# The gating branch's v projection as seven block products, with block sums of its weights made by accumulating transfers

## The chip, the core and the metric

The kernel runs on one core of a Trainium2 chip. The core's engines work side by side and meet through semaphores: TensorE (PE) does the matmuls and transposes, ScalarE (ACT) and VectorE (DVE) work on tiles in SBUF and PSUM, GpSimd (POOL) builds masks and issues accumulating transfers, and SyncE (SP) issues loads. The metric is the device time of one execution in microseconds (us); lower is better. All inputs and outputs are float32.

## The reference, cut to what matters

One decoder layer for 512 tokens of width 1024: one input projection of x feeds a gated branch (gMLP) and a sparse attention of three branches, both are projected and merged, and a channel mixer with two layer norms follows. What the change touches is the gated branch's v:

```
z = x @ w_in                        # columns 0:1024 are u, 1024:2048 are v
u, v = split(gelu(z[:, :2048]), 2)
v = layer_norm(v, gm_ln_g, gm_ln_b) # then a causal 128 x 128 mix over positions, per group
y_gm = u * (W_s v + b)
...
k_cmp, v_cmp = compress(z_kc), compress(z_vc)    # the stage that follows v
f = square(relu(h @ w_ff1)) @ w_ff2              # made with seven products for 3 of 4 quarters
```

## The kernel before

**Precision.** Each float32 matmul is three matmuls on split operands. `split` (L142) makes a hi part of a weight tile on ACT (L150) and the remainder lo on DVE (L151); `xh` and `xl` are the same split of x^T, made out of PSUM after PE's transposes (L339 to L344). A product is hi x hi, hi x lo and lo x hi.

**The weight stream.** `Stream` (L40 to L98) holds two lists: chunks, which are loads into a ring of buffers (L80, issued by SP), and items, which are splits of a chunk or of a part of it. A chunk's load can be issued once the last item of the chunk that held its buffer has been split. The ring `raw` has two buffers; the hi and lo tiles have three each. `ws.get` hands out the next item and prepares two more ahead. Rings `V` and `S`, in a pool that opens only for the channel mixer, serve FF2.

**The order of the work.** The program is written in the order of the stages; around v that is: x transposed and u's first six columns (L347 to L366, order written out by hand), u's last two columns (L372 to L378), v (L403 to L418), small transposes of constants (L432 to L441), the projections kc and vc (L442 to L451), the compression (L454 to L460). Outside the parts under `manual_schedule` a scheduler places the instructions of each engine in an order of its own, fixed when the kernel is built; on the chip each engine then runs its list strictly in order and waits where an operand or a buffer is late.

**v.** Two column halves of 512. For each, eight contraction blocks k times four token tiles t, with x^T's 128 x 128 blocks stationary and 512 weight columns moving, three matmuls each: 2 x 8 x 4 x 3 = 192 matmuls into four PSUM banks. ACT evicts with gelu into `v`, DVE collects `bn_stats`. The weights come as eight chunks of 512 KB, each split in one go. After v, ACT issues the loads of the compression's weights, `cw1_0` and `cw1_1`, 2 MB each (L420 to L423); constants for the gated branch (`gmc`, three rows spread over all partitions, and `misc`) are loaded from ACT's queue while u ends (L385 to L398).

**FF2.** For three of the four quarters of w_ff2, `du_chunks`, `du_item` and `s13` (L211 to L248) make seven products out of blocks. The weight is cut into blocks W(k, c), contraction half k and column half c, each further into two parts h. Chunk U holds W11 and W22, V holds W21, S holds W12 twice. `s13` adds U to both copies of S; later S is added to U and U to V. Each addition is a transfer of 512 KB from SBUF to SBUF that POOL issues with `accum_op=add` (L207). `ff2_product` (L854) multiplies in the order 1, 2, 6, 5, 7, 3, 4 and adds each product's bank into `hn`.

**Masks.** The attention pool `apool` opens at the start; POOL makes the distance masks `Bm` and `Dc` in it, and ACT scales `Bm`'s four slices during u (L365).

Of the kernel before, what the change touches and what calls it, by code (L numbers as in the profile page):

```python
# [16 lines left out]
P = 128  # L17
# [83 lines left out]
def layer_kernel(ctx: ExitStack, tc: tile.TileContext, x, w_in, gm_ln_g, gm_ln_b, gm_w_s, gm_b_s,  # L101
# [66 lines left out]
    def rows_b(src, ks, c0, ncol, per_piece=1, dst=None):  # L168
        for k in ks[::2]:
# [5 lines left out]
    add(**dict(shape=[1, 768], dmas=[(lambda t: t, wv[:, 0:1, 0:768])],  # L175
                       pieces=[((lambda t, j=j: t[:, 0, 384 * j:384 * j + 384]), None) for j in range(2)]))
    add(**dict(shape=[1, 768], dmas=[(lambda t: t, wv[:, 1:2, 0:768])],
                       pieces=[((lambda t: t[:, 0]), None)]))
    rows_b(wv, list(range(2, 8)), 0, 768)
    cols_a(w_in, 768, 256)  # L180
    for h in range(2):
        rows_b(wv, list(range(8)), C_V + 512 * h, 512, per_piece=2)
    cols_a(w_in, C_KC, 512)
    cols_a(w_in, C_KS, 256)
    cols_a(w_in, C_KW, 256)
    for k in range(0, 8, 2):
        add(**dict(
            shape=[2, 536],
            dmas=[(lambda t: t[:, :, 0:256], wv[:, k:k + 2, C_VS:C_VS + 256]),
                  (lambda t: t[:, :, 256:536], wv[:, k:k + 2, C_VW:C_VW + 280])],  # L190
            pieces=[((lambda t, j=j: t[:, j]), None) for j in range(2)]))
    cols_a(w_pg, 0, 1024)
    cols_a(w_in, C_Q, 1024)
    cols_a(w_in, C_ZM, 2048)
    cols_a(w_pn, 0, 1024)
    res = {}
    w_ov = w_o.rearrange("(k p) c -> p k c", p=P)
    rows_b(w_ov, [0, 1], 0, 1024)
    rows_b(w_ov, [2, 3, 4, 5], 0, 1024, dst=lambda k: (res["oh"][:, k - 2], res["ol"][:, k - 2]))
    rows_b(w_ov, [6, 7], 0, 1024)  # L200
    w2v = w2.rearrange("(k p) c -> p k c", p=P)
    w1v = w1.rearrange("(k p) c -> p k c", p=P)
    for name in "VS":
        ws.ring(name, 2, lambda shape, n, tag=name: res["lpool"].tile([P] + shape, F32, tag=tag, bufs=2, name=n),
                ready=lambda: "rings" in res)
# [5 lines left out]
    def du_chunks(shape, blk):  # L211


        one, two = (lambda t: t[:, 0]), (lambda t: t[:, 1])
        return dict(U=ws.chunk("raw", [2] + shape, [(two, blk(0, 0)), (one, blk(1, 1))]),
                    V=ws.chunk("V", shape, [((lambda t: t), blk(0, 1))]),
                    S=ws.chunk("S", [2] + shape, [(one, blk(1, 0)), (two, blk(1, 0))]))

    def ff2_blocks(q, h):
        def blk(half, k):  # L220
            k0 = 8 * q + 4 * k + 2 * h
            return w2v[:, k0:k0 + 2, 512 * half:512 * half + 512]
        return du_chunks([2, 512], blk)
# [25 lines left out]
    FF2 = (1, 2, 6, 5, 7, 3, 4)  # L249
# [11 lines left out]
    for q in range(4):  # L261
        for i, c in enumerate((0, 512, 256, 768)):
            cols_a(w1, 1024 * q + c, 256, ring="S" if q and i < 2 else "raw",
                   dsts=((early, early if i == 0 else None) if q == 0 and i < 2 else (None, None)))
        if q < 3:
            dus = [ff2_blocks(q, h) for h in range(2)]
            for p in FF2:
                for h in range(2):
                    du_item(dus[h], p, s13(dus[h]) if p == 1 else None)
# [15 lines left out]
    for c, (c0, c1) in enumerate(((0, 128), (128, 256), (256, 512), (512, 768), (768, 1024))):  # L285
# [3 lines left out]
    att = ctx.enter_context(ExitStack())  # L289
    apool = att.enter_context(tc.tile_pool(name="apool", bufs=1))  # L290
    Kh = apool.tile([P, 2, 1056], F32R, name="Kh")
    Kl = apool.tile([P, 2, 1056], F32R, name="Kl")
    Vch = apool.tile([32, 2, HD], F32R, name="Vch")
    Vcl = apool.tile([32, 2, HD], F32R, name="Vcl")
    Bm = apool.tile([P, 4, 512], F32, name="Bm")
    Dm = Bm[:, 0]
    nc.gpsimd.iota(Dm, pattern=[[-1, 512]], base=384, channel_multiplier=1,
                   allow_small_or_imprecise_dtypes=True)
    nc.gpsimd.affine_select(Dm, Dm, pattern=[[-1, 512]], compare_op=ALU.is_ge, fill=BIG,
                            base=384, channel_multiplier=1)  # L300
    Dc = apool.tile([P, 4, 32], F32, name="Dc")
    nc.gpsimd.iota(Dc, pattern=[[128, 4], [-16, 32]], base=-15, channel_multiplier=1,
                   allow_small_or_imprecise_dtypes=True)
    nc.vector.tensor_scalar(Dc, Dc, -0.5, None, op0=ALU.add)
    nc.gpsimd.affine_select(Dc, Dc, pattern=[[128, 4], [-16, 32]], compare_op=ALU.is_ge, fill=BIG,
                            base=-31, channel_multiplier=1)
# [30 lines left out]
    uT = slab("uT", [P, 8, S])  # L337

    def x_transpose(k):  # L339
        pt = bank("d")  # L340
        for t in range(4):
            nc.tensor.transpose(pt[:, t * P:(t + 1) * P], xn[:, t, k * P:(k + 1) * P], ident)
        nc.scalar.activation(xh[:, k], pt, AF.Copy)
        nc.vector.tensor_sub(xl[:, k], pt, xh[:, k].bitcast(F32))  # L344

    ub = [bank(t) for t in BANKS[:6]]
    with tc.manual_schedule():  # L347
        ws.prep(0)
        x_transpose(0)
        for k in range(8):  # L350
            if k == 0:
# [12 lines left out]
            if k in (3, 4, 5, 6):  # L364
                nc.scalar.activation(Bm[:, 6 - k], Dm, AF.Copy, scale=2.0 ** (k - 7))  # L365
    for c in range(6):  # L366
        nc.scalar.activation(uT[:, c], ub[c], AF.Gelu_apprx_tanh)

# [5 lines left out]
    for c in range(6, 8):  # L374
        pc = ws.get()
        ps = bank("d")
        dense_a(ps, pc, xh, xl)
        nc.scalar.activation(uT[:, c], ps, AF.Gelu_apprx_tanh)  # L378

# [24 lines left out]
    for h in range(2):  # L404
        vb = [bank(t) for t in (BANKS[:4] if h == 0 else BANKS[4:])]
        for kk in range(4):
            hi, lo = ws.get()
            for j in range(2):
                k = 2 * kk + j
                for t in range(4):  # L410
                    ts_ = slice(t * P, (t + 1) * P)
                    nc.tensor.matmul(vb[t], xh[:, k, ts_], hi[:, j], start=k == 0, stop=False)  # L412
                    nc.tensor.matmul(vb[t], xl[:, k, ts_], hi[:, j], start=False, stop=False)  # L413
                    nc.tensor.matmul(vb[t], xh[:, k, ts_], lo[:, j], start=False, stop=k == 7)  # L414
        for t in range(4):
            vs_ = v[:, t, h * 512:(h + 1) * 512]
            nc.scalar.activation(vs_, vb[t], AF.Gelu_apprx_tanh)
            nc.vector.bn_stats(st6[:, t, h], vs_)  # L418
    cw1 = []
    for i, w in enumerate((cmp_w1_k, cmp_w1_v)):  # L420
        t = slab(f"cw1_{i}", [P, 32, HD])
        nc.scalar.dma_start(t, w[0].rearrange("(l d) e -> d l e", d=HD))
        cw1.append(t)  # L423

# [379 lines left out]
    def block(t, i):  # L804
        return t[:, i].rearrange("p (k t) -> p k t", k=4)

# [47 lines left out]
    def ff2_product(q, p):  # L854

        where = {1: "A", 2: "B", 5: "C", 6: "A", 3: "C", 7: "A", 4: "A"}[p]
        opens = p in (1, 2, 5)
        if opens:
            g2[where] = [bank(t) for t in {"A": "dd", "B": "aa", "C": "ac"}[where]]
        for h in range(2):  # L860
            hi, lo = ws.get()
            for j in range(2):
                js = slice(j * P, (j + 1) * P)
                ps = g2[where][j]
                for kk in range(2):
                    yh, yl = (y[:, 2 * h + kk, js] for y in Y[p])
                    nc.tensor.matmul(ps, yh, hi[:, kk], start=opens and h == 0 and kk == 0, stop=False,  # L867
                                     skip_group_check=True)
                    nc.tensor.matmul(ps, yl, hi[:, kk], start=False, stop=False, skip_group_check=True)  # L869
                    nc.tensor.matmul(ps, yh, lo[:, kk], start=False, stop=h == 1 and kk == 1,  # L870
                                     skip_group_check=True)
        half, e, sign, first = {1: (0, 0, 1, 1), 2: (0, 0, 1, 0), 6: (1, 0, 1, 1), 5: (1, 1, -1, 1),
                                7: (1, 1, -1, 0), 3: (1, 0, 1, 0), 4: (0, 1, -1, 1)}[p]
        for j in range(2):
            v = hn[:, 2 * half + j, e * 512:(e + 1) * 512]
            nc.vector.scalar_tensor_tensor(v, v, ALPHA if q == 0 and first else 1.0, g2[where][j],
# [7 lines left out]
    for q in range(4):  # L884
# [17 lines left out]
        if q < 3:  # L902
            for p in FF2:
                ff2_product(q, p)
# [44 lines left out]
```

## Time and profile before

| what | us |
|---|---|
| median of 3 runs | 893.12 |
| lowest, highest run | 891.62, 894.25 |
| the profiled execution, its own time | 893.99 |
| its span in the trace | 892.3 |
| u, its first and last matmul's start | 7.45, 55.35 |
| v, its first and last matmul's start | 55.58, 98.87 |
| small transposes, the first one's start | 99.19 |
| kc, its first matmul's start | 100.27 |

The span runs from the first to the last recorded instruction; the time of the execution is a little longer. A matmul's recorded duration (0.39 us) is longer than its distance to the next one, because matmuls overlap in the array: rates are read from the starts.

### The profile page before, as it was taken

To read this page: it belongs to the slowest core of one execution; us is meant where nothing else is said; L and a number is where in the kernel's file an instruction comes from. 1 tells how busy PE (TensorE), PEld (TensorE's weight loads), DVE (VectorE), ACT (ScalarE), POOL (GpSimd) and SP (SyncE) were. 2 spreads that over 40 slices of the span, in tenths; PEclk is the share of its full clock that TensorE was granted. 3 is DMA by queue.
4 is the path that set the end of the run, shared out by engine and by line. 5 is a ranking of instruction groups with operands and counts; after the bars stand their busy time and mean duration, and the time that the engine had idled before them with its cause. 6 is when DMAs were issued, how large, how long until landed. Compare 5 with 4: busy or idle time off the path is not lost.

```text
span 892.3 us, 10986 instructions
## 1 busy us (share of the span) xinstructions
PE 878.0 (98%) x4288; PEld 734.0 (82%) x4288; DVE 500.4 (56%) x977; ACT 367.8 (41%) x644; POOL 24.3 (3%) x36
## 2 busy tenths in 40 slices
PE   8999999999999999999999999999999999999995
PEld 6888898998888788888878888888888888888884
DVE  3423654542236866766745688457457635853457
ACT  3522322342234655656633412554355345535500
POOL 1000000000000000000000000010011001100000
PEclk9999999999999999999999999999999999999998
DMA  6467520143331111121135441666557738541401
GB/s 203 127 196 204 175 72 25 51 157 100 106 100 57 48 48 48 48 94 49 41 118 195 165 142 42 194 147 183 188 148 136 235 125 183 114 146 48 142 24 71
DMA packets 70772, 104.78 MB, mean 117 GB/s; under 512 B 2432, under 2 KB 50368, under 8 KB 70720
## 3 DMA queue, kind: packets, MB, share of 16 engines
q1 hardware_dynamic: 62752, 83.99, 29.1%
q0 software_dynamic: 3456, 12.58, 7.5%
q10 hardware_dynamic: 4512, 7.50, 2.7%
q8 instruction: 33, 0.54, 0.3%
q14 instruction: 19, 0.16, 0.0%
HBM read 89.39 MB, written 2.10 MB: 103 GB/s over the span
## 4 chain that ended last, share of the span: by engine, by line
PE 97%; DVE 1%; DMA 1%; ACT 0%; issue 0%; SPq 0%; DVEq 0%; ACTq 0%
PE ps L133 19%; PE ps L135 19%; PE ps L134 19%; PE ps L867 4%; PE ps L870 4%; PE ps L869 4%; PE ps L737 3%; PE ps L735 3%; PE ps L736 3%; PE ps L662 2%; PE ps L414 2%; PE ps L412 2%; PE ps L457 2%; PE ps L413 2%; PE ps L677 1%; PE ps L679 1%
## 5 line engine op out<-in xcount | busy, mean ns | idle before, releaser
L151 DVE TENSOR_TENSOR wlo<-raw,whi 128x1024 fp32r<-128x1024 f32 (+3 forms) x118 | 136.6, 1162 | 196.2 <-ACT whi L150 192.7
L150 ACT ACTIVATE whi<-raw 128x1024 fp32r<-128x1024 f32 (+3 forms) x118 | 118.9, 1011 | 234.2 <-PE ps L134 154.1
L133 PE MATMUL ps<-xh,whi 128*128 128x512 f32 x320 | 129.4, 404 | 0.0
L135 PE MATMUL ps<-xh,wlo 128*128 128x512 f32 x320 | 125.8, 393 | 0.0
L134 PE MATMUL ps<-xl,whi 128*128 128x512 f32 x320 | 125.8, 393 | 0.0
L133 PE MATMUL ps<-hTh,whi 128*128 128x512 f32 x232 | 90.3, 389 | 0.0
L134 PE MATMUL ps<-hTl,whi 128*128 128x512 f32 x232 | 90.3, 389 | 0.0
L135 PE MATMUL ps<-hTh,wlo 128*128 128x512 f32 x232 | 90.3, 389 | 0.0
L135 PEld LDWEIGHTS ps<-xh,wlo 128*128 128x128 f32 x320 | 60.5, 189 | 13.2
L134 PEld LDWEIGHTS ps<-xl,whi 128*128 128x128 f32 x320 | 60.6, 190 | 9.5
L133 PEld LDWEIGHTS ps<-xh,whi 128*128 128x128 f32 x320 | 60.6, 190 | 9.4
L867 PE MATMUL ps<-whi,y 128*128 128x512 f32 x168 | 65.5, 390 | 0.0
L870 PE MATMUL ps<-wlo,y 128*128 128x512 f32 x168 | 65.5, 390 | 0.0
L869 PE MATMUL ps<-whi,y 128*128 128x512 f32 x168 | 65.5, 390 | 0.0
L135 PEld LDWEIGHTS ps<-hTh,wlo 128*128 128x128 f32 x232 | 43.6, 188 | 9.1
L134 PEld LDWEIGHTS ps<-hTl,whi 128*128 128x128 f32 x232 | 43.5, 188 | 9.0
L133 PEld LDWEIGHTS ps<-hTh,whi 128*128 128x128 f32 x232 | 43.6, 188 | 8.9
L621 ACT ACTIVATE PP<-PP,nm 128x512 f32<-128x512 f32 (+3 forms) x64 | 35.8, 560 | 35.5 <-DVE nm L615 35.2
L150 ACT ACTIVATE whi<-S 128x1024 fp32r<-128x1024 f32 x24 | 25.6, 1065 | 48.4 <-PE ps L869 35.3
L151 DVE TENSOR_TENSOR wlo<-S,whi 128x1024 fp32r<-128x1024 f32 x24 | 29.4, 1225 | 25.1 <-ACT whi L150 25.1
L830 DVE TENSOR_TENSOR y<-RR,y 128x512 fp32r<-128x512 f32 x50 | 33.1, 689 | 16.0 <-ACT y L829 16.0
L870 PEld LDWEIGHTS ps<-wlo,y 128*128 128x128 f32 x168 | 31.5, 188 | 6.8
(210 smaller groups left out, 1671.6 us busy)
## 6 DMA issues: line engine op xcount, KB each, us to landing
raw<-in_w_in_dram SPq DMA_DIRECT2D x17, 1024.0 KB, 5.2
raw<-in_w_ff_dram SPq DMA_DIRECT2D x14, 1024.0 KB, 5.5
raw<-in_w_ff_dram SPq DMA_DIRECT2D x12, 512.0 KB, 4.1
S<-in_w_ff_dram SPq DMA_DIRECT2D x12, 512.0 KB, 4.4
S<-raw POOLq DMA_DIRECT2D x12, 512.0 KB, 5.8
S<-in_w_ff_dram SPq DMA_DIRECT2D x6, 1024.0 KB, 5.5
raw<-in_w_in_dram SPq DMA_DIRECT2D x8, 512.0 KB, 3.7
raw<-in_w_proj_gm_dram SPq DMA_DIRECT2D x4, 1024.0 KB, 5.0
```

The lines of the kernel that those rows point to most:

```text
L133: nc.tensor.matmul(ps, hi, mh, start=start, stop=False)
L134: nc.tensor.matmul(ps, hi, ml, start=False, stop=False)
L135: nc.tensor.matmul(ps, lo, mh, start=False, stop=stop)
L150: nc.scalar.activation(hi, r, AF.Copy)
L151: nc.vector.tensor_sub(lo, r, hi.bitcast(F32))
L621: nc.scalar.activation(t, t, AF.Exp, bias=nm[:, e, i:i + 1], scale=-1.0, accum_out=sm[:, e, i:i + 1])
L735: nc.tensor.matmul(ps, th, hi[:, cs], start=start, stop=False)
L736: nc.tensor.matmul(ps, tl, hi[:, cs], start=False, stop=False)
L830: nc.vector.tensor_sub(Y[c][1][:, rows], t, Y[c][0][:, rows].bitcast(F32))
L867: nc.tensor.matmul(ps, yh, hi[:, kk], start=opens and h == 0 and kk == 0, stop=False, skip_group_check=True)
L869: nc.tensor.matmul(ps, yl, hi[:, kk], start=False, stop=False, skip_group_check=True)
L870: nc.tensor.matmul(ps, yh, lo[:, kk], start=False, stop=h == 1 and kk == 1, skip_group_check=True)
```

## The change

v is computed from blocks as FF2 is: x^T in four blocks (contraction half by token half of 256), v's weights in four blocks, seven products of 24 matmuls instead of eight. With X(k,t) the block of contraction half k and token half t, the products are 1: X(1,1) W11; 2: X(2,1) W21; 6, 5, 7 and 4: combinations of x blocks with W11+W12+W22, W12+W22, W11+W12 and W22; 3: X(2,2) with the sum of all four weight blocks. Products 1, 6, 7 and 4 add up in one pair of PSUM banks, 5 and 3 in another, 2 has its own.

- `x_transpose` makes a third copy `xT` on ACT. `x_blocks` makes the four combinations in place on DVE and splits them into `x56` and `x74` (ACT and DVE). It is written behind u's column 6.
- The weights come as two units (parts h = 0 and 1) of U (two loads of 512 KB into a `raw` buffer), V (512 KB) and S (512 KB twice): 5 MB where it was 4 MB, and eight accumulating transfers from POOL. V and S have rings `v` and `s` of their own, in a pool `rpool` that is open from the start to the end of v; they may load from u's step k = 4 on. A split now serves 12 matmuls instead of 24: 14 splits instead of 8.
- U keeps its two `raw` buffers until product 4, v's last, so the loads of the kc columns wait for that.
- Evictions: a copy, a negated copy, or an addition on DVE with gelu after it.
- `apool` opens behind v; POOL's masks and ACT's four `Bm` copies move there. `cw1_0` is loaded behind product 7 and `cw1_1` behind v.
- `products` is the former loop of `ff2_product`; `unit`, `du_chunks`, `du_item` and `s13` are moved up and shared.

```diff
...
+    ORDER = (1, 2, 6, 5, 7, 3, 4)
+    for name in "VSvs":
+        pool = "lpool" if name < "a" else "rpool"
...
+    def unit(src, k0, c0, rings="VS"):
+
+        def blocks(h):
+            def blk(half, k):
+                r = k0 + 4 * k + 2 * h
+                return src[:, r:r + 2, c0 + 512 * half:c0 + 512 * half + 512]
+            return du_chunks([2, 512], blk, rings)
+        dus = [blocks(h) for h in range(2)]
+        for p in ORDER:
+            for h in range(2):
+                du_item(dus[h], p, s13(dus[h]) if p == 1 else None)
...
-    for h in range(2):
-        rows_b(wv, list(range(8)), C_V + 512 * h, 512, per_piece=2)
+    unit(wv, 0, C_V, "vs")
...
         nc.scalar.activation(xh[:, k], pt, AF.Copy)
+        nc.scalar.activation(xT[:, k], pt, AF.Copy)
...
+            if k == 4:
+                res["begun"] = True
...
-            if k in (3, 4, 5, 6):
-                nc.scalar.activation(Bm[:, 6 - k], Dm, AF.Copy, scale=2.0 ** (k - 7))
...
+    def x_split(p, src):
+        nc.scalar.activation(X[p][0], src, AF.Copy)
+        nc.vector.tensor_sub(X[p][1], src, X[p][0].bitcast(F32))
+
+    def x_blocks():
+        b11, b12, b21, b22 = (xT[:, k:k + 4, c:c + 256] for k in (0, 4) for c in (0, 256))
+        nc.vector.tensor_sub(b11, b11, b12)
+        nc.vector.tensor_sub(b12, b22, b12)
+        nc.vector.scalar_tensor_tensor(b22, b11, -1.0, b22, op0=ALU.mult, op1=ALU.subtract)
+        nc.vector.scalar_tensor_tensor(b21, b22, -1.0, b21, op0=ALU.mult, op1=ALU.subtract)
+        for p, src in ((6, b22), (5, b11), (7, b12), (4, b21)):
+            x_split(p, src)
...
+    def products(get, Y, p, g, tags):
...
+        for h in range(2):
+            hi, lo = get()
+            for j in range(2):
+                js = slice(j * P, (j + 1) * P)
+                ps = g[where][j]
+                for kk in range(2):
+                    yh, yl = (y[:, 2 * h + kk, js] for y in Y[p])
+                    nc.tensor.matmul(ps, yh, hi[:, kk], start=opens and h == 0 and kk == 0, stop=False,
+                                     skip_group_check=True)
...
+    for p in ORDER:
+        ps = products(ws.get, X, p, vg, {"A": "aa", "B": "ab", "C": "bc"})
+        half, e = {1: (0, 0), 2: (0, 0), 6: (1, 0), 5: (1, 1), 7: (1, 1), 3: (1, 0), 4: (0, 1)}[p]
+        for j in range(2):
+            t = 2 * half + j
+            vs_ = v[:, t, e * 512:(e + 1) * 512]
+            if p in (1, 6):
+                nc.scalar.activation(vs_, ps[j], AF.Copy)
+            elif p == 5:
+                nc.scalar.activation(vs_, ps[j], AF.Copy, scale=-1.0)
+            elif p == 4:
+                nc.scalar.activation(vs_, ps[j], AF.Gelu_apprx_tanh, scale=-1.0)
+            else:
+                nc.vector.tensor_tensor(vs_, vs_, ps[j], op=ALU.subtract if p == 7 else ALU.add)
+                nc.scalar.activation(vs_, vs_, AF.Gelu_apprx_tanh)
...
+        if p == 7:
+            cw_load(0, cmp_w1_k)
+    early_pool.close()
...
```

**Order, POOL, from the start to FF2's first additions, before.** `Bm`, `Dc` and `rowok` are masks, `misc` holds gm_w_s, S and raw are FF2's chunks.

```order
L299 AFFINE_SELECT Bm<-Bm 128x512
L302 IOTA Dc 128x128
L309 AFFINE_SELECT rowok<-rowok 128x1
L305 AFFINE_SELECT Dc<-Dc 128x128
L399 AFFINE_SELECT misc<-misc 128x1024
L208 DMA S_4457<-raw_4707 128x1024 x2
L208 DMA S_4460<-raw_4781 128x1024
```

**The same stretch now.** raw_360 and raw_400 are the U chunks of h = 0 and 1, s_270, s_273 and v_266, v_268 the S and V chunks.

```order
L298 AFFINE_SELECT rowok<-rowok 128x1
L185 DMA s_270<-raw_360 128x1024 x2
L185 DMA s_273<-raw_400 128x1024 x2
L185 DMA raw_360<-s_270 128x1024
L185 DMA raw_400<-s_273 128x1024
L420 AFFINE_SELECT misc<-misc 128x1024
L185 DMA v_266<-raw_360 128x1024
L185 DMA v_268<-raw_400 128x1024
L484 IOTA Bm 128x512
L489 IOTA Dc 128x128
L486 AFFINE_SELECT Bm<-Bm 128x512
L492 AFFINE_SELECT Dc<-Dc 128x128
```

Six of the eight additions stand one behind the other; the addition into raw_360 (h = 0) comes behind both S additions of h = 1, the mask of `misc` in front of the V additions, and the distance masks behind all of them.

**Order, DVE, around v's end, before.** raw_637 and raw_667 are the chunks of kc and vc, raw_565 and raw_607 the last of v, ps_737 and ps_741 the first small transposes.

```order
L151 TENSOR_TENSOR wlo_610<-raw_565,whi_609 128x1024
L151 TENSOR_TENSOR wlo_640<-raw_607,whi_639 128x1024
L151 TENSOR_TENSOR wlo_670<-raw_637,whi_669 128x1024
L151 TENSOR_TENSOR wlo_698<-raw_637,whi_697 128x1024
L418 BN_STATS st_113<-v 128x6 x2
L446 BN_AGGR mv<-st_113 128x2
L418 BN_STATS st_113<-v 128x6
L435 COPY misc<-ps_737 128x32
L435 COPY misc<-ps_741 128x32
```

**The same place now.** v_266 and v_268 are the V chunk (product 3), raw_360 and raw_400 the U chunks (product 4), ps_491, ps_492 and ps_603, ps_604 the banks of products 7 and 3, ps_782 and ps_786 the first small transposes.

```order
L469 TENSOR_TENSOR v<-v,ps_491 128x512
L469 TENSOR_TENSOR v<-v,ps_492 128x512
L509 COPY misc<-ps_782 128x32
L509 COPY misc<-ps_786 128x32
L151 TENSOR_TENSOR wlo_656<-v_268,whi_655 128x1024
L472 BN_STATS st_98<-v 128x6 x2
L151 TENSOR_TENSOR wlo_680<-raw_360,whi_679 128x1024
L151 TENSOR_TENSOR wlo_698<-raw_400,whi_697 128x1024
L469 TENSOR_TENSOR v<-v,ps_603 128x512
L469 TENSOR_TENSOR v<-v,ps_604 128x512
```

Before, the splits of kc's chunk (raw_637) stand ahead of the copies of the small transposes; now the copies stand ahead of the splits of products 3 and 4, and kc's splits come later than all of these rows.

**Order, ACT, around v's end, before.** ps_603 to ps_606 are the banks of v's second half.

```order
L150 ACTIVATE whi_609<-raw_565 128x1024
L150 ACTIVATE whi_639<-raw_607 128x1024
L422 DMA cw_1_735<-in_cmp_w_v_dram 128x32x128
L150 ACTIVATE whi_669<-raw_637 128x1024
L150 ACTIVATE whi_697<-raw_637 128x1024
L417 ACTIVATE v<-ps_603 128x512
L417 ACTIVATE v<-ps_604 128x512
L417 ACTIVATE v<-ps_605 128x512
L150 ACTIVATE whi_759<-raw_667 128x1024
L417 ACTIVATE v<-ps_606 128x512
```

**The same place now.** raw_695 is kc's chunk, raw_719 vc's, ps_491 and ps_492 are product 4's banks.

```order
L470 ACTIVATE v<-v 128x512 x2
L150 ACTIVATE whi_679<-raw_360 128x1024
L150 ACTIVATE whi_697<-raw_400 128x1024
L495 ACTIVATE Bm<-Bm 128x512 x4
L470 ACTIVATE v<-v 128x512 x2
L467 ACTIVATE v<-ps_491 128x512
L150 ACTIVATE whi_721<-raw_695 128x1024
L150 ACTIVATE whi_737<-raw_695 128x1024
L467 ACTIVATE v<-ps_492 128x512
L452 DMA cw_1_780<-in_cmp_w_v_dram 128x32x128
```

Before, both splits of kc's chunk stand ahead of v's last four evictions; now they stand behind the first of product 4's two evictions, and the four `Bm` copies ahead of it.

## Rows read from the trace of the kernel before

**Rows 1.** Page parts 1 and 4: busy us by engine; chain by engine.

```profile
PE 878.0 (98%) x4288; PEld 734.0 (82%) x4288; DVE 500.4 (56%) x977; ACT 367.8 (41%) x644; POOL 24.3 (3%) x36
...
PE 97%; DVE 1%; DMA 1%; ACT 0%; issue 0%; SPq 0%; DVEq 0%; ACTq 0%
```

**Rows 2.** PE's waits in the whole span: total us, times, longest us.

```profile
PE ps L342 <- DMA xn<-in_x_dram: 2.3, 1, 2.3
PE ps L134 <- DVE hTl L792: 0.7, 1, 0.7
```

**Rows 3.** Timeline, v's ends: start us, us, engine line op out<-in xcount.

```profile
55.58 0.39 PE L412 MATMUL ps<-whi,xh 128*128 128x512 f32 x1
...
98.87 0.39 PE L414 MATMUL ps<-wlo,xh 128*128 128x512 f32 x1
...
99.86 0.27 DVE L435 COPY misc<-ps 128x32 f32<-128x32 f32 x2
...
100.27 0.48 PE L133 MATMUL ps<-xh,whi 128*128 128x512 f32 x1
```

**Rows 4.** PE's timeline, first and last matmul of FF2's first unit.

```profile
594.30 0.39 PE L867 MATMUL ps<-whi,y 128*128 128x512 f32 x1
...
632.31 0.39 PE L870 MATMUL ps<-wlo,y 128*128 128x512 f32 x1
```

**Rows 5.** Groups by line and form: busy us, mean ns of one.

```profile
L151 DVE TENSOR_TENSOR wlo<-raw,whi 128x1024 fp32r<-128x1024 f32 x101 | 123.1, 1224 | 179.1 <-ACT whi L150 175.8 <-DMA raw<-in_w_ff_dram 3.2
...
L418 DVE BATCH_NORM_STATS2 st<-v 128x6 f32<-128x512 f32 x8 | 5.3, 686 | 3.8 <-ACT v L417 3.8
...
L150 ACT ACTIVATE whi<-raw 128x1024 fp32r<-128x1024 f32 x101 | 106.8, 1061 | 218.1 <-PE ps L134 150.8 <-PE ps L413 16.1 <-PE ps L869 13.3
...
L417 ACT ACTIVATE v<-ps 128x512 f32<-128x512 f32 x8 | 4.6, 596 | 4.6 <-PE ps L414 4.4
```

**Rows 6.** Windows: busy us (xcount) by engine, PE clock, DMA share, GB/s.

```profile
10.00:20.00 10.00, 10.00 (x46) 8.17 (x45) 2.57 (x5) 2.67 (x4) 0.00 (x0) 0.91 0.65 238
40.00:50.00 10.00, 10.00 (x46) 8.29 (x45) 3.26 (x5) 5.49 (x8) 0.00 (x0) 1.00 0.80 261
```

**Rows 7.** Timeline: the load into U0's buffer, and u's last split on DVE.

```profile
39.05 0.37 SPq L80 DMA_DIRECT2D raw<-in_w_in_dram  x1
...
41.69 1.23 DVE L151 TENSOR_TENSOR wlo<-raw,whi 128x1024 fp32r<-128x1024 f32 x1 [0.92 <-ACT whi L150]
```

**Rows 8.** Transfers, 583 to 585 us (loads alone): packets, MB, share of 16 engines.

```profile
q1 hardware_dynamic: 391, 0.77, 102.9%
```

**Rows 9.** Transfers, 587 to 594.5 us (additions alone).

```profile
q0 software_dynamic: 397, 1.50, 106.3%
```

**Rows 10.** Issues from 597.7 us: one addition, KB, us to landing.

```profile
raw<-S POOLq DMA_DIRECT2D x1, 512.0 KB, 4.5
```

**Rows 11.** Transfers, 573.5 to 575.5 us (additions and loads together).

```profile
q0 software_dynamic: 84, 0.34, 84.9%
q1 hardware_dynamic: 74, 0.14, 21.6%
```

**Rows 12.** Issues, whole span: xcount, KB each, median us to landing.

```profile
raw<-in_w_in_dram SPq DMA_DIRECT2D x17, 1024.0 KB, 5.2
...
raw<-in_w_ff_dram SPq DMA_DIRECT2D x12, 512.0 KB, 4.1
...
cw<-in_cmp_w_k_dram ACTq DMA_DIRECT2D x1, 0.5 KB, 11.9
```

**Rows 13.** Transfers and issues, 79 to 83 us.

```profile
q10 hardware_dynamic: 591, 1.21, 103.4%
...
raw<-in_w_in_dram SPq DMA_DIRECT2D x1, 1024.0 KB, 13.4
```

**Rows 14.** PE's timeline after the wait on x: two matmuls.

```profile
8.53 0.63 PE L134 MATMUL ps<-xl,whi 128*128 128x512 f32 x1
...
11.87 0.40 PE L133 MATMUL ps<-xh,whi 128*128 128x512 f32 x1
```

More of the change, by code (lines that the diff above doesn't have):

```diff
@@ L173, in rows_b @@
                         for j in range(2)] if per_piece == 1 else [((lambda t: t), None)]))
[L175 to L180, printed above, removed]
-    for h in range(2):
-        rows_b(wv, list(range(8)), C_V + 512 * h, 512, per_piece=2)
[L183 to L195, printed above, removed]
-    res = {}
[L197 to L205, printed above, removed]
+    res = {}
+    ORDER = (1, 2, 6, 5, 7, 3, 4)
+    for name in "VSvs":
+        pool = "lpool" if name < "a" else "rpool"
+        ws.ring(name, 2, lambda shape, n, tag=name, pool=pool: res[pool].tile([P] + shape, F32, tag=tag, bufs=2,
+                                                                            name=n),
+                ready=lambda key="rings" if name < "a" else "begun": key in res)
     def dma_add(dst, src):
@@ L209, in dma_add, with du_chunks @@
                             accum_op=ALU.add)
-    def du_chunks(shape, blk):
+    def du_chunks(shape, blk, rings="VS"):
         one, two = (lambda t: t[:, 0]), (lambda t: t[:, 1])
         return dict(U=ws.chunk("raw", [2] + shape, [(two, blk(0, 0)), (one, blk(1, 1))]),
[L216 to L223, printed above, removed]
+                    V=ws.chunk(rings[0], shape, [((lambda t: t), blk(0, 1))]),
+                    S=ws.chunk(rings[1], [2] + shape, [(one, blk(1, 0)), (two, blk(1, 0))]))
+    def unit(src, k0, c0, rings="VS"):
[8 more added lines that the diff above has]
+                du_item(dus[h], p, s13(dus[h]) if p == 1 else None)
     def du_item(d, p, pre=None):
@@ L265, in layer_kernel @@
         if q < 3:
[L266 to L269, printed above, removed]
+            unit(w2v, 8 * q, 0)
     rows_b(w2v, [24, 25], 0, 1024)
@@ L287, in layer_kernel @@
     ws.load(2)
[L289 to L306, printed above, removed]
+    early_pool = ctx.enter_context(ExitStack())
+    res["rpool"] = early_pool.enter_context(tc.tile_pool(name="rpool", bufs=1))
     rowok = small.tile([P, 1], F32, name="rowok")
@@ L378, in layer_kernel @@
         nc.scalar.activation(uT[:, c], ps, AF.Gelu_apprx_tanh)
+        if c == 6:
+            x_blocks()
     gmc = slab("gmc", [P, 4, D])
@@ L403, in layer_kernel, with cw_load @@
     v = slab("v", [P, 4, D])
[L404 to L407, printed above, removed]
-            for j in range(2):
[L409 to L418, printed above, removed]
+    def products(get, Y, p, g, tags):
+        where = {1: "A", 2: "B", 5: "C", 6: "A", 3: "C", 7: "A", 4: "A"}[p]
+        opens = p in (1, 2, 5)
+        if opens:
+            g[where] = [bank(t) for t in tags[where]]
+        for h in range(2):
+            hi, lo = get()
+            for j in range(2):
+                js = slice(j * P, (j + 1) * P)
[4 more added lines that the diff above has]
+                                     skip_group_check=True)
+                    nc.tensor.matmul(ps, yl, hi[:, kk], start=False, stop=False, skip_group_check=True)
+                    nc.tensor.matmul(ps, yh, lo[:, kk], start=False, stop=h == 1 and kk == 1,
+                                     skip_group_check=True)
+        return g[where]
     cw1 = []
-    for i, w in enumerate((cmp_w1_k, cmp_w1_v)):
+    def cw_load(i, w):
         t = slab(f"cw1_{i}", [P, 32, HD])
@@ L854, in ff2_product @@
     def ff2_product(q, p):
[L856 to L871, printed above, removed]
+        ps = products(ws.get, Y, p, g2, {"A": "dd", "B": "aa", "C": "ac"})
         half, e, sign, first = {1: (0, 0, 1, 1), 2: (0, 0, 1, 0), 6: (1, 0, 1, 1), 5: (1, 1, -1, 1),
@@ L875, in ff2_product @@
             v = hn[:, 2 * half + j, e * 512:(e + 1) * 512]
-            nc.vector.scalar_tensor_tensor(v, v, ALPHA if q == 0 and first else 1.0, g2[where][j],
+            nc.vector.scalar_tensor_tensor(v, v, ALPHA if q == 0 and first else 1.0, ps[j],
                                            op0=ALU.mult, op1=ALU.add if sign > 0 else ALU.subtract)
@@ L902, in layer_kernel @@
         if q < 3:
-            for p in FF2:
+            for p in ORDER:
                 ff2_product(q, p)
```

63 lines of the change are left out of this document (60 added, 3 removed).

## The prediction

> **What bounds the kernel now.** I read the page's head and its chain first [rows 1]: TensorE (PE) is busy for 98% of the span and carries 97% of the chain that ended last. The list of PE's waits comes next [rows 2]: besides the start (2.3 us on x there) it holds 0.7 us in front of the channel mixer as its largest entry, and nothing in v. So the time is the row of PE's matmuls. A matmul that goes is worth its distance to the next one, and work elsewhere costs only what it makes PE wait. Third, PE's timeline around v [rows 3]: v's 192 matmuls start at 55.58, the last at 98.87, so 0.2266 us apart; ten small transposes follow, and the first matmul of the compressed keys (kc) starts at 100.27, 1.2 us after v's last has made room. Below, t counts from v's first matmul. Fourth, what the new loop costs is to be seen in FF2, which already runs the same seven products [rows 4]: 168 matmuls from 594.30 to 632.31, 0.2276 apart, without a wait. Last come the durations of ScalarE (ACT) and VectorE (DVE) [rows 5] and then the transfers, because what is new beside PE is transfers and order.
>
> **Removed.** 192 matmuls at 0.2266 are 43.5 us; 168 at 0.2276 are 38.2 us. PE's row gets 5.3 us shorter. Everything below is taken off that.
>
> **Work before v.** Eight copies of x^T (0.60 each, like the eviction of that size) join ACT, four copies of Bm leave it. The x blocks are four combinations and four lo parts on DVE, 8 x 1.22 = 9.8 us, and four hi parts on ACT, 4 x 1.06 = 4.2 us [rows 5]. They fall before 56 us, where DVE is busy a third and ACT half of the time [rows 6]. PE there runs u, which waits for neither. I cost them at nothing; u's last two columns (48 matmuls, 10.9 us) hide them, and without that cover the first combined block would be late for product 6 at t = 10.9. They delay one thing: a U chunk is loaded when DVE has split the piece that held its buffer. U0's load was issued at 39.05; one combination in front makes that 40.2. U1's waits for u's last piece, split at 42.92 [rows 7]; two combinations, partly in idle time, make that about 43.7.
>
> **The accumulating transfers, and product 6.** Product 6 needs W11 + W12 + W22: two additions, one after the other, for each half h. POOL's order has both S additions of h = 0, both of h = 1, and only then U += S of h = 0; what is queued behind them is the V additions, needed much later. The trace gives three rates: a weight load alone moves 0.77 MB in 2.0 us, 2.7 us for 1 MB [rows 8]; additions alone keep all 16 engines full at 1.50 MB in 7.5 us, 2.6 us each [rows 9], with 4.5 us from issue to landing [rows 10], so some 1.3 to start and 0.6 to the signal; and side by side the additions hold 85% of the engines, the loads 22% [rows 11]. U0's two 512 KB loads (4.1 each [rows 12], the second issued 0.4 later) are down at 44.8, so additions move data from about 46.2. Needed: product 6 starts at 55.58 + 48 x 0.2276 = 66.5; its third matmul reads the lo part, so with 1.06 + 1.22 for the split the fifth addition has to be down by 64.5, the sixth by 67.2. Lower end: additions undisturbed, 46.2 + 5 x 2.6 + 0.6 = 59.8, no wait. Upper end: everything queued since 45 goes first, one 1 MB chunk (2.7), the four 512 KB constants of ACT's queue (4 x 1.4) and five additions (13.1): 68.5, 4.0 us late. Between them by the shares of [rows 11]: two additions beside one loading queue (80% left, 3.3 each) to 52.8, three beside two such queues (66%, 3.95 each) to 64.7, down at 65.3, 0.8 late; the sixth follows at about 68.7, 0.7 more. I take 1.5 us of waiting, the end nearest to that row, and keep 0 and 4.0.
>
> On this the Trainium skill (DMA: Bandwidth & Descriptors, section Queues, rings and completion order) says that a DMA engine goes round the queues that have work, one packet each. The row's packet counts, 84 against 74, agree. With three queues it would give the additions one turn in three instead of my 66% of the time; as an estimate from the same row, the wait would be near 2.6 us and the sum 1.1 us worse.
>
> **The end of v, and kc.** Before, kc's first piece was split before v's last evictions: its rows stand ahead of them on ACT, and PE went from v through the transposes to kc without a wait [rows 3]. Now U0 keeps its raw buffer until the last product, so kc's 1 MB load can start only when product 4's first piece is split. In DVE's order that split stands behind two copies of the small transposes, and these PE runs after 11 of the 14 pieces, t = 11 x 12 x 0.2276 = 30.0. Then: copies to 30.7 (0.27 for both [rows 3]); lo of piece 12, 1.22, to 32.0; two bn_stats of 0.69 [rows 5] to 33.3; lo of product 4's first piece to 34.6. There SP issues the load; it takes 5.2 us [rows 12], so it is down at 39.8; hi is ready at 40.9. PE has finished v and the transposes at t = 14 x 12 x 0.2276 + 1.2 = 39.4. Wait: 1.5 us. PE's order then has two matmuls of the first piece and two of the second, whose hi comes 1.0 us after the first one's: another 0.5 us. Together 2.0 us; I take 1.9, since PE changes between matmuls and transposes more often than before and so comes a little later. Lower end, if the load were early: ACT's order puts this split behind product 4's first eviction (PE done at 38.3, gelu 0.60), so hi is not ready before 40.0, and 1.1 us remain. Upper end: the load takes what loads of that size took beside a cw chunk, 13.4 us instead of 5.2 [rows 12, 13]: 8.2 us more, 10.1. I take the lone load's row, because the V additions are long done and the only large transfer near is cw_0, whose issue follows product 5 (t about 22): at the 1.21 MB in 4 us of [rows 13] its 2.1 MB take 7 us and some 2 to start, to t = 31 to 33.
>
> **The attention pool's opening.** Iota, select and Bm's four copies now stand behind v: 2.5 us of ACT ahead of the last evictions, done by t = 36 and needed at 38.3. Nothing. From kc's second pair of matmuls on, the orders of all engines are those of before.
>
> **Sum.** -5.3 + 1.5 + 1.9 = -1.9 us on the profiled execution's 893.99 (span 892.3 and 1.7 around it): 892.1. The median of the runs shown, 893.12, lies 0.9 below that execution; I predict the median: 891.2.
>
> **Rivals.**
> A. Both waits near their lower ends: additions in time, kc's load no obstacle. 0.0 to 0.4 and 1.1 to 1.9, so -3.0 to -4.2 on the median: 888.9 to 890.1. For it: FF2 runs the same unit without any wait [rows 2, 4]. Against it: there U is loaded over 10 us earlier before the products, and the next stage's chunk has a ring of its own.
> B. Slower: the additions fall behind. Place: product 6, on the fifth addition. If the engines stay shared until everything is done, the wait is 4.0, and from a wait of about that length a second price comes: after the 2.3 us wait at the start eight spacings, 8.53 to 11.87, took 3.3 us instead of 1.8 [rows 14], and the granted clock of the stretch from 10 us reads 0.91 [rows 6], which is time at the lower of the two levels (1.2 instead of 2.4 GHz): 1.5 us. -5.3 + 4.0 + 1.5 + 1.9 = +2.1: 895.2. It becomes slower than before once the two waits and the clock exceed 5.3 us. For it: additions fill the engines by themselves [rows 9], and six of them, a chunk and the constants are 15.7 + 2.7 + 5.6 = 24 us of transfers in the 22 us from 45 to 67. Against: the constants are not needed early, and the additions get the larger share. The Trainium skill (TensorE: Matmul & The Clock Gate, part 1) has idling followed by the half clock as its rule; [rows 14] agree.
> C. Slower or level: kc's load meets cw_0. It decides when cw_0 is still moving at t = 34.6, that is when it takes over 11 us instead of 9; it took 11.9 before, beside other loads [rows 12]. Price: 4 to 8 us more, 895 to 899. Against: nothing else should be loading then.
> D. That v is not made by seven products is not a rival; the instruction list shows 168.
>
> **How the numbers follow.** A measurement of this kernel tells about 0.3% from no change, 2.7 us: faster means below 890.4, slower above 895.8. My forecast (both waits, 890.1 to 892.4) gets 0.45: 0.11 of it faster, 0.34 the same. A gets 0.30, all faster. B gets 0.14: 0.05 slower, 0.09 the same. C gets 0.11: 0.09 slower, 0.02 the same. Together: faster 0.41, same 0.45, slower 0.14. The range reaches from a little below A (888.5) to B's 895.2 and leaves out C's worst; the forecast's own is 890.1 to 892.4.
>
> **What would show it.** PE's waits after: one at product 6 (a new line of the product loop, on ACT's hi or DVE's lo, itself behind a POOL transfer) of 0 to 4 us, and one at the kc line of 1.1 to 2 us behind a load issued at t = 34 to 35; 168 matmuls 0.227 to 0.228 apart between the two. A wait in u, or at product 1 or 2, would mean that the x blocks or the 3 MB of early V and S loads cost what I put at nothing. If the kc wait is on the load and long, C; if PE's clock falls behind product 6, B; if neither wait is there, A, and my ordering of the transfers is wrong.

## The result and the profile after

The changed kernel takes 898.92 us (897.52 to 899.49, four runs), the kernel before 893.33 (891.62 to 894.25, four runs): ratio 1.0057, 95% interval 1.0045 to 1.007. Forecast were 891.2 us and a range of 888.5 to 895.2, so the change is slower, and by more than the range allowed. The execution profiled here has a span of 897.8 us, against 892.3 before.

First PE's waits in the whole span (total, times, longest), the list that holds nothing in v before [rows 2]:

```profile
PE ps L441 <- ACT whi L150: 5.2, 1, 5.2
PE ps L332 <- DMA xn<-in_x_dram: 2.6, 2, 2.1
PE ps L133 <- ACT whi L150: 1.4, 2, 1.2
```

L441 is the first matmul of the product loop, and its one wait is as long as the gain that was to be had. L133 is kc. PE's timeline shows where the wait is: v's first matmul, the last of product 1, product 2 from its first matmul on, v's last matmul, and kc.

```profile
56.00 0.39 PE L441 MATMUL ps<-whi,xh 128*128 128x512 f32 x1
...
61.21 0.39 PE L444 MATMUL ps<-wlo,xh 128*128 128x512 f32 x1
66.81 0.79 PE L441 MATMUL ps<-whi,xh 128*128 128x512 f32 x1 [5.21 <-ACT whi L150]
67.40 0.63 PE L443 MATMUL ps<-whi,xl 128*128 128x512 f32 x1
...
72.09 0.57 PE L441 MATMUL ps<-whi,xh 128*128 128x512 f32 x1
72.50 0.39 PE L443 MATMUL ps<-whi,xl 128*128 128x512 f32 x1
...
103.23 0.39 PE L444 MATMUL ps<-wlo,x 128*128 128x512 f32 x1
...
104.96 0.50 PE L133 MATMUL ps<-xh,whi 128*128 128x512 f32 x1 [1.22 <-ACT whi L150]
```

Product 2 waits 5.21 us, and the next twelve spacings, 66.81 to 72.09, take 5.28 us instead of 12 x 0.2276 = 2.73. The windows (busy us of PE, PEld, DVE, ACT and POOL with counts, then the granted clock, DMA share, GB/s) name the reason: the clock is at its lower level, 1.2 instead of 2.4 GHz, behind the idle stretch.

```profile
61.00:66.00 5.00, 0.60 (x3) 0.18 (x1) 0.00 (x0) 0.30 (x1) 0.05 (x1) 0.96 1.09 261
66.00:72.00 6.00, 5.19 (x12) 3.99 (x13) 4.45 (x3) 3.74 (x5) 2.76 (x3) 0.50 0.81 162
```

The first window also shows that from 61 to 66 nearly nothing works on the core but the DMA engines, and these are full. PE waits for whi, so for ACT; and ACT, by its timeline (ACTq is its issuing of a DMA), was not computing either:

```profile
52.42 1.44 ACTq L416 DMA_DIRECT2D misc<-in_gm_w_s_dram  x1
56.20 0.60 ACT L397 ACTIVATE uT<-ps 128x512 f32<-128x512 f32 x1 [3.89 <-PE ps L135]
56.20 3.24 ACTq L418 DMA_DIRECT2D misc<-in_cmp_w_k_dram  x1
59.48 2.42 ACTq L419 DMA_DIRECT2D misc<-in_cmp_pe_k_dram  x1
61.94 0.57 ACTq L418 DMA_DIRECT2D misc<-in_cmp_w_v_dram  x1
62.55 3.10 ACTq L419 DMA_DIRECT2D misc<-in_cmp_pe_v_dram  x1
65.70 2.00 ACT L150 ACTIVATE whi<-v 128x1024 fp32r<-128x1024 f32 x2 [8.90 <-issue]
```

Four loads of 16 and 64 KB keep ACT 9.3 us, only to be issued, and product 2's two splits stand behind them on ACT. In the kernel before the same four issues stood ahead of a split too, took 0.44 to 0.60 us each, and no matmul waited:

```profile
50.77 0.60 ACTq L397 DMA_DIRECT2D misc<-in_cmp_w_k_dram  x1
51.41 0.44 ACTq L398 DMA_DIRECT2D misc<-in_cmp_pe_k_dram  x1
51.88 0.45 ACTq L397 DMA_DIRECT2D misc<-in_cmp_w_v_dram  x1
52.36 0.47 ACTq L398 DMA_DIRECT2D misc<-in_cmp_pe_v_dram  x1
```

What is new beside them are the additions. From 60 to 65 us, by queue (packets, MB, share of 16 engines), the additions are q0 and ACT's constants q10; the last line is the issue of the fifth addition, with its time to landing:

```profile
q0 software_dynamic: 165, 0.57, 57.7%
q10 hardware_dynamic: 1101, 0.79, 50.2%
...
raw<-s POOLq DMA_DIRECT2D x1, 512.0 KB, 8.5
```

The engines are full with the two together, and the gating weights' load (L416, 512 KB in pieces of 512 bytes) lands 17.4 us after its issue. The fifth addition, issued at 60.21, is down at 68.7: later than the 64.5 at which the prediction wanted it for product 6.

**The budget.** From the first matmul of v to the last: 43.29 us before, 47.23 after. The experiments show 39.07 for the seven products where nothing is late (the small transposes, which came behind v before, lie inside it), so 8.16 us are lost in v: 5.21 of recorded waiting and 2.95 more, of which 2.55 are the twelve spacings at the lower clock. Against the removed 5.3 us stand these 8.2 and the wait in front of kc, 1.2 to 1.4: from v's first matmul to kc's first it is 48.96 us instead of 44.69, +4.3. v opens 0.4 us later, and that difference is already there at the second column's transposes (13.24 before, 13.66 after), so it is the start's. The last 0.8 us of the 5.5 between the spans lie behind kc's first matmul: 0.5 of it in kc's first few matmuls, around its second wait of 0.22 (the third recorded one starts 0.95 behind the first, 0.55 before); for the remaining 0.3 I have no cause.

### The profile page after: what moved, and what is told of

It reads as the page before. It is cut to its first block, busy times and chain, and to the rows that moved or that the text cites. A ratio compares the mean times of both kernels' runs of the same rounds, so it can differ in the third digit from the quotient of the medians.

```text
span 897.8 us, 11033 instructions
## 1 busy us (share of the span) xinstructions
PE 876.7 (98%) x4264; PEld 731.1 (81%) x4264; DVE 520.9 (58%) x997; ACT 384.3 (43%) x668; POOL 31.1 (3%) x44
## 4 chain that ended last, share of the span: by engine, by line
PE 95%; DMA 1%; DVE 1%; ACTq 1%; ACT 1%; issue 0%; SPq 0%; DVEq 0%
PE ps L133 19%; PE ps L134 19%; PE ps L135 19%; PE ps L441 5%; PE ps L444 5%; PE ps L443 5%; PE ps L811 3%; PE ps L810 3%; PE ps L809 3%; PE ps L736 2%; PE ps L531 2%; PE ps L751 1%; PE ps L753 1%; PE ps L752 1%; PE ps L594 1%; PE ps L596 1%
## 5 line engine op out<-in xcount | busy, mean ns | idle before, releaser
L150 ACT ACTIVATE whi<-raw 128x1024 fp32r<-128x1024 f32 (+3 forms) x116 | 116.7, 1009 | 201.2 <-PE ps L134 142.1
L133 PE MATMUL ps<-xh,whi 128*128 128x512 f32 x320 | 129.6, 405 | 1.4 <-ACT whi L150 1.4
L133 PE MATMUL ps<-hTh,whi 128*128 128x512 f32 x232 | 90.3, 389 | 0.0
L133 PEld LDWEIGHTS ps<-xh,whi 128*128 128x128 f32 x320 | 60.7, 190 | 11.6 <-ACT whi L150 2.2
L441 PE MATMUL ps<-whi,y 128*128 128x512 f32 x168 | 65.5, 390 | 0.0
L133 PEld LDWEIGHTS ps<-hTh,whi 128*128 128x128 f32 x232 | 43.5, 188 | 9.0
L443 PEld LDWEIGHTS ps<-whi,y 128*128 128x128 f32 x168 | 31.5, 188 | 6.8
```

The costliest lines, as they stand in the source:

```text
L133: nc.tensor.matmul(ps, hi, mh, start=start, stop=False)
L150: nc.scalar.activation(hi, r, AF.Copy)
```

## The experiments

The theory, T1: the additions and ACT's constants fill the DMA engines together; ACT's queue backs up, its issues take 2 to 3 us each, and product 2's split is held behind them. The rivals: the additions alone are late whatever ACT does; the gating weights' small pieces alone do it; the new work ahead of v (x blocks) does it; the constants cost the kernel before as well.

**The four small loads moved behind the splits.**

```diff
-    for i, (w, pe) in enumerate(((cmp_w2_k, cmp_pe_k), (cmp_w2_v, cmp_pe_v))):
-        nc.scalar.dma_start(w2s[i], w[0])
-        nc.scalar.dma_start(pes[i], pe[0])
...
+        if p == 5:
+            for i, (w, pe) in enumerate(((cmp_w2_k, cmp_pe_k), (cmp_w2_v, cmp_pe_v))):
+                nc.scalar.dma_start(w2s[i], w[0])
+                nc.scalar.dma_start(pes[i], pe[0])
```

> The changed kernel with the four small constant loads (second compressor weights and position rows) issued from ScalarE behind product 5 instead of ahead of product 2's splits; nothing else is moved. Theory T1 (in the changed kernel these four issues took 3.24, 2.42, 0.57 and 3.10 us because the DMA engines were full with accumulating transfers, and product 2's split stood behind them on ScalarE): the 5.2 us wait at product 2 and the half clock behind it (some 2.6 us) go, and the next late thing is product 6: its U1 needs the fifth addition, which landed at 68.7 in the changed kernel, and the sixth, at 72.8, while product 6 is due at 66.9. So 2 to 3 us of wait for the fifth and about 1 more for the sixth come in place of the 5.2; some of that is saved if the additions finish sooner: 893 to 897 against 898.9. Rival R1 (only ScalarE's place was wrong, the additions are in time): no wait at product 6, 898.9 - 7.8 = 891. Rival R2 (the split of product 2 is late for its data or its buffers, not for the issues): the wait stays, 898 to 899.

897.36 us (ratio to before 1.0045, 1.0031 to 1.0058). In ACT's order the loads came out directly behind product 2's splits, not as late as the text has them, which is enough for the question. PE's waits in the product loop:

```profile
PE ps L438 <- ACT whi L150: 3.5, 1, 3.5
PE ps L441 <- DVE wlo L151: 1.0, 1, 1.0
```

and ACT's timeline, the first split of product 2 and of product 6:

```profile
57.26 1.05 ACT L150 ACTIVATE whi<-v 128x1024 fp32r<-128x1024 f32 x1
...
69.99 1.06 ACT L150 ACTIVATE whi<-raw 128x1024 fp32r<-128x1024 f32 x1 [5.66 <-DMA raw<-s]
```

Product 2's wait is gone, which shows that the issues made it. But 4.5 us of waiting now stand at product 6, behind the fifth and sixth additions, with 3.1 us more, most of it lower clock (v takes 46.60: 39.07 + 4.47 + 3.06). So ACT's held stream cost little of its own: v is 0.6 us shorter than in the changed kernel, the medians lie 1.6 us apart, and the two ratio intervals overlap. The lateness of the additions lay beneath it. The time is just above the 893 to 897 that I expected, which had no lower clock behind the new wait.

**Without v's additions.**

```diff
 def dma_add(dst, src):
+        if "att" not in res:
+            return
...
     early_pool.close()
+    res["att"] = True
```

> The changed kernel without v's eight accumulating transfers (the products then use the plain blocks; FF2's additions stay). T1: ScalarE's seven issues take 0.35 to 0.6 us each as before, landings fall from 8 to 17 us to some 4 to 7, no wait at products 2 or 6, 891. Rival R5 (it is the gating weights' 512-byte pieces that back ScalarE's queue up, with or without additions): issues of 2 to 3 us and a wait of 3 to 5 us at product 2 stay, 896 to 899.

891.29 us (0.9973, 0.9964 to 0.9982). ACT's four issues:

```profile
56.00 0.35 ACTq L420 DMA_DIRECT2D misc<-in_cmp_w_k_dram  x1
56.38 0.44 ACTq L421 DMA_DIRECT2D misc<-in_cmp_pe_k_dram  x1
56.85 0.45 ACTq L420 DMA_DIRECT2D misc<-in_cmp_w_v_dram  x1
57.34 0.44 ACTq L421 DMA_DIRECT2D misc<-in_cmp_pe_v_dram  x1
```

and PE's waits, apart from the start:

```profile
PE ps L133 <- ACT whi L150: 1.4, 2, 1.1
PE ps L134 <- DVE hTl L869: 0.6, 1, 0.6
```

Without the additions the gating weights' small pieces hold nobody up, so that rival falls in this form. v takes 39.07 us. The x blocks, their copies and the attention pool's move are all still in, and nothing in u or v waits for them: u takes 42.32 us, 42.34 before. The time stands next to the forecast's 891.2 by chance: that sum holds 1.5 us of waiting at product 6, which this run does not have.

**The gating weights alone moved.** (POOL's mask that reads them moves with them, behind the last addition.)

```diff
-    nc.scalar.dma_start(wsr, gm_w_s[0].rearrange("g i j -> i g j"))
...
+        if p == 5:
+            nc.scalar.dma_start(wsr, gm_w_s[0].rearrange("g i j -> i g j"))
```

> The changed kernel with the gating weights alone (1024 pieces of 512 bytes, landing 17.4 us after the issue) moved behind product 5; the four small loads stay ahead of product 2's split. If the backlog of this one load in ScalarE's queue is what holds the four issues (T1b), they take 0.4 to 0.6 us each, product 2's wait is gone and what is left is product 6's wait as in the first of these runs: 893 to 896. If the additions alone hold them (T1a), two or three of the four still take over 2 us and the wait at product 2 is 3 to 5 us: 896 to 899.

897.48 us (1.0041, 1.0029 to 1.0054), in the range of T1a, but with issues mostly between the two: with 512 KB less in ACT's queue the same four issues take

```profile
52.32 1.36 ACTq L417 DMA_DIRECT2D misc<-in_cmp_w_k_dram  x1
56.14 0.34 ACTq L418 DMA_DIRECT2D misc<-in_cmp_pe_k_dram  x1
56.52 1.20 ACTq L417 DMA_DIRECT2D misc<-in_cmp_w_v_dram  x1
57.75 1.46 ACTq L418 DMA_DIRECT2D misc<-in_cmp_pe_v_dram  x1
```

three of them neither 0.4 to 0.6 (T1b) nor over 2 (T1a). That range was met by luck: T1a's wait of 3 to 5 us at product 2 did not come. Product 2 is in time and product 6 waits, as T1b had it; v takes 45.31 us.

```profile
PE ps L438 <- ACT whi L150: 2.4, 1, 2.4
PE ps L441 <- DVE wlo L151: 1.3, 1, 1.3
```

So the issues grow shorter without this load in ACT's queue. How the queue holds an issue back, and whether the bytes, the pieces or the pace of what stands in it set the length, these runs do not show.

**All constants ahead of the additions.** All seven loads are issued in u, at k = 2.

```diff
+    def constants():
+        nc.scalar.dma_start(gmg, bcast(gm_ln_g[0]))
...
+            if k == 2:
+                constants()
```

> The changed kernel with all seven constant loads (2.2 MB: the three broadcast rows, the gating weights, the four small ones) issued from ScalarE in u at k = 2 (about 20 us), where the DMA share is 0.23; none is left beside the additions. T1: no issue stands ahead of product 2's split, and the additions, which shared the engines with 2.2 MB of constants, land some 5 us sooner: waits at products 2 and 6 both gone, 898.9 - 5.2 - 2.6 = 891.1, a wait of 1.4 us at kc left. Rival R3 (the additions are late by themselves, 5.2 MB at some 200 GB/s are 15 us behind an issue at 46.2): a wait of 1 to 4 us at product 6 with half clock behind it, 892.5 to 896. Rival R4 (the constants now delay u's own loads): a wait in u, 891 plus that wait.

893.38 us (1.0004, 0.9995 to 1.0013). v runs in 39.07 us with all its additions and without a wait: the rival that the additions are too slow by themselves (R3) falls. (Its 5.2 MB do not fit its 15 us, they are 26 us at 200 GB/s; the five additions up to the one that product 6 waits for are 2.6 MB, 13 us.) What the run loses it loses in u, where the bunched issues held ACT's next split:

```profile
21.85 0.91 ACTq L347 DMA_DIRECT2D misc<-in_cmp_w_k_dram  x1
22.80 1.03 ACTq L348 DMA_DIRECT2D misc<-in_cmp_pe_k_dram  x1
...
24.95 0.84 ACT L150 ACTIVATE whi<-raw 128x768 fp32r<-128x768 f32 x1 [3.90 <-issue]
```

and PE waited for it (the longest of these three waits; the other two, 0.90 and 0.22, are at kc):

```profile
PE ps L133 <- ACT whi L150: 2.5, 3, 1.4
```

This is the wait in u that R4 named, but ACT's issues make it and not late loads. From the second column's transposes to v's opening u takes 44.48 us there, 42.34 in the kernel before and in the changed one. So four large loads of its own ahead of them slow ACT's issues as well, though less: 0.91 and 1.03 us, then 0.51 and 0.49.

**The constants spread.** Two of the loads at each of k = 1, 2, 3 and 4.

```diff
-    def constants():
+    def constants(k):
+        if k == 1:
             nc.scalar.dma_start(gmg, bcast(gm_ln_g[0]))
             nc.scalar.dma_start(gmb, bcast(gm_ln_b[0]))
+        elif k == 2:
...
-            if k == 2:
-                constants()
+            constants(k)
```

> The changed kernel with the seven constant loads issued two at a time at k = 1 to 4 of u. In the run where all seven stood at k = 2, v ran without a wait (39.07 us from its first matmul to its last, as in the run without additions), but ScalarE was held by the issues from 19.97 to 24.95 us, and u took 44.48 us from the second column's transposes to v's opening, against 42.34 in the changed kernel and in the kernel before. If the issues' bunching is what cost those 2.1 us, they come back: 893.4 - 2.1 = 891.3. Rival: the constants' 2.2 MB hold up u's own loads wherever they stand (the DMA share is about 1 from 10 to 16 us): 0.5 to 2 us of wait in u stay, 892 to 893.5.

890.98 us, ratio 0.997 (0.9959 to 0.998): near the expected 891.3, and 0.3% faster than the kernel before. PE's timeline, v's first and last matmul and kc:

```profile
55.55 0.39 PE L448 MATMUL ps<-whi,xh 128*128 128x512 f32 x1
...
94.62 0.39 PE L451 MATMUL ps<-wlo,x 128*128 128x512 f32 x1
...
96.19 0.50 PE L133 MATMUL ps<-xh,whi 128*128 128x512 f32 x1 [1.06 <-ACT whi L150]
```

No issue of a constant takes over 0.49 us, and u takes its 42.32 us. POOL's issue of the fifth addition, and its time to landing:

```profile
55.37 0.84 POOL L185 DMA_DIRECT2D raw<-s  x1 [5.15 <-DMA s<-raw]
```

```profile
raw<-s POOLq DMA_DIRECT2D x1, 512.0 KB, 6.8
```

It is down at 62.2 where the changed kernel had 68.7 and 64.5 is needed. Only the constants have moved.

**The control.** The same spread in the kernel before.

```diff
+    def constants(k):
...
+            constants(k)
             if k > 0:
                 pcs = [ws.get(1 if k < 7 else 2)]
```

> The kernel before the change, with only the constants' issues spread over u as above. Theory: no additions run beside them there, the four small issues took 0.44 to 0.60 us each and no matmul waited for them, so nothing is gained: 893.5, within 0.5 us of before. Rival: the constants cost the kernel before too (for instance in kc or u), so that part of the gain of the other two runs is theirs alone: 891 to 892.5.

893.76 us (1.0004, 0.9995 to 1.0013): nothing. The constants' place matters only beside the additions, and the gain of the run above belongs to the seven products.

**The wait at kc.** Spread constants, and v's last products in another order, so that the first U chunk is free one product sooner. (Products 5 and 7 change places in the evictions with it.)

```diff
+    ORDER_V = (1, 2, 6, 7, 5, 4, 3)
...
-        chunks = {1: "US", 2: "VU", 5: "S", 6: "US", 3: "VU", 7: "S", 4: "U"}[p]
+        chunks = {1: "US", 2: "VU", 5: "S", 6: "US", 3: "V", 7: "S", 4: "U"}[p]
...
-    unit(wv, 0, C_V, "vs")
+    unit(wv, 0, C_V, "vs", ORDER_V)
```

> The kernel with spread constants, and v's products in the order 1, 2, 6, 7, 5, 4, 3 instead of 1, 2, 6, 5, 7, 3, 4 (FF2's stay): the first chunk U is done with one product, 5.45 us, sooner, so the first kc load is issued that much sooner. Theory: the kc wait (0.90 to 1.22 and 0.2 us in all runs) is the load issued at product 4's last split and landing 5.2 to 5.4 us later, so it goes: 1.1 to 1.4 us less than the run with spread constants alone, about 890. Rival: kc's first split is late because ScalarE and VectorE are at v's last evictions, not for its load: the wait stays, 891.3; or product 4 now waits for product 7's eviction from the bank it adds to: up to 1 us more.

890.55 us, ratio 0.9965 (0.9952 to 0.9977), the fastest measured, though not told apart from the run before it. PE's timeline, product 3 (now the last) and kc:

```profile
93.94 0.50 PE L453 MATMUL ps<-wlo,xh 128*128 128x512 f32 x1 [0.55 <-DVE wlo L151]
...
95.67 0.39 PE L453 MATMUL ps<-wlo,xh 128*128 128x512 f32 x1
95.90 0.40 PE L133 MATMUL ps<-xh,whi 128*128 128x512 f32 x1
```

kc follows v at a matmul's distance, so its wait was the load's, as forecast. Of the 1.3 us of waiting little remains as gain, 0.25 us from v's first matmul to kc's (40.39 instead of 40.64): product 3's lo part now comes late on DVE, behind the copies of the small transposes, which PE runs in front of it.

## Why the prediction was wrong

**The step that failed** is the part on the accumulating transfers and product 6: "I take 1.5 us of waiting, the end nearest to that row, and keep 0 and 4.0." It was too small by five times, and its place was wrong. Three things in it failed. The first of them rests on these rows of the changed kernel: the queues from 45 to 50 us (no packet of q0, the additions' queue, is among them), then q0 from 50 to 55 and from 55 to 60.

```profile
q1 hardware_dynamic: 602, 1.13, 70.1%
q10 hardware_dynamic: 82, 0.34, 25.6%
...
q0 software_dynamic: 228, 0.87, 88.2%
...
q0 software_dynamic: 189, 0.68, 68.3%
```

1. The start of the additions, and their order. The middle value had them moving data from 46.2, one behind the other, the second done by 52.8 and the fifth down at 65.3. The first addition, issued at 46.20, moved its first packet between 50.2 and 50.4: the loads and ACT's first constant had the engines until then. From there on the shares were near those that I took from [rows 11] (80 and 66%). But the additions did not go one by one: the second landed 12.8 us after an issue at about 47.2, so at 60, when q0 had moved 1.55 MB, as much as three additions. The fifth was issued only then, at 60.21, and was down at 68.7. This lies next to the step's upper end, 68.5 (whose terms, taken from 46.2, add up to 68.2), in part by chance: the gating weights, which that end lets go first, landed at 69.8. Taking the constants out of the way brings the fifth to 62.2, between the lower end (59.8) and the middle.
2. The 4.0 us was kept as the end of the term without the lower clock behind it, which only rival B had (1.5 us, from [rows 14]). Beside waits of 5.2, 4.5 and 3.8 us in v, in the changed kernel and in the runs with the small loads and with the gating weights moved, v is longer by another 2.95, 3.06 and 2.5: in the changed kernel the first twelve spacings took about double, where I had read eight.
3. "The constants are not needed early" was said of their data, against rival B. Their issues are instructions of ACT, and product 2's splits stand behind them. I priced these transfers as bytes on the engines only; a transfer's issue is also time on the engine that issues it, and that time grew from 0.5 to as much as 3.24 us. The document's own sign, "a wait in u, or at product 1 or 2", was the one that came, from a cause I had not listed.

Rival B was right in kind (additions fill the engines, PE idles, the clock falls) and had a chance of 0.14; its place, product 6, is where the wait stands once product 2's is gone, and by its sum 4.0 + 1.5 = 5.5 stand where 8.2 were lost.

The rule that was weighed there, that engines go round the queues with work (DMA: Bandwidth & Descriptors, section Queues, rings and completion order, of the Trainium skill), would have given 2.6 us of wait, which is nearer to the 4.5 at product 6 than my 1.5. The packets that the profile counts from 60 to 65 us, 165 of q0 against 1101 of q10, are not one for one; whether they speak against the rule stays open, since a packet of that section can hold several descriptors and no run here shows what the profile counts as one. The same page, section Issuing engines are not separate DMA queues, says that issuing from several engines saves only the sequencer's time to initiate a transfer, "which is usually small relative to the DMA itself". This case agrees on the shared engines (57.7% and 50.2% of the same 16 from 60 to 65 us); the time to initiate, 3.24 us of the 13.8 that a 64 KB load took from issue to landing, was not small here.

**The steps that held.** Removed, -5.3: with nothing late (spread constants) v's opening to kc's first matmul takes 40.64 us against 44.69 before, -4.05, which is -5.3 with 1.06 of kc's wait, to 0.2. Work before v, nothing: u takes 42.34 us in both kernels. The pool's opening, nothing: no wait shows it. The kc wait, 1.9 (1.1 to 10.1): 1.4 us, of 1.22 and 0.22 (1.7 with the 0.5 that the starts show behind the first), in the place named; the load was issued at 98.39, t = 42.4, which less the 8.2 us lost in v is 34.2 (forecast 34.6), and took 5.4 us (forecast 5.2). Rival C did not come: cw_0 was down before. These steps alone add up to -3.4 us. The run with spread constants shows -3.3 in its span (889.0 against 892.3) and a ratio that means -2.7 (-1.8 to -3.7); the run without additions -2.4 (-1.6 to -3.2), a little less than the sum. That both medians, 891.29 and 890.98, stand beside the forecast of 891.2 is luck: without its 1.5 us at product 6 the forecast is 889.7, and the kernel before measured 893.80 and 894.11 beside these runs, not the 893.12 that I started from.

## What to carry to other kernels

When a change adds transfers to a stretch, list every DMA issue that stands in the stream of an engine whose results PE waits for, and ask what stands behind it there; with full DMA engines an issue of 0.4 us can become one of 3. Move constants and other small loads out of such a stretch before judging the change: here that turned +0.6% into -0.3%. A wait can hide a second one that shows only once the first is removed (here 5.2 us at product 2 hid 4.5 at product 6), and to a wait of several us in front of PE the lower clock behind it has to be added.

## What had not been expected of the hardware

The issue of one of the four small loads from ACT took 0.35 to 0.60 us in the kernel before and in the run without additions, 0.49 to 1.03 behind 2 MB of ACT's own loads, and 3.24, 2.42, 0.57 and 3.10 beside the additions and the gating weights; product 2's split, behind them in ACT's stream, started only when the last was done. An addition can also start late: in the changed kernel 4 us passed from the first one's issue to its first packet, with the constants spread, beside the same loads, 2 us (45.87 to about 48). From 60 to 65 us 1101 packets of ACT's queue, most of them the gating weights' pieces of 512 bytes, moved 0.79 MB in 50% of the engines' time while 165 of the additions moved 0.57 MB in 58%.
